# A hybrid decoder layer on one core: the output projection reads its activations by token halves, in pairs of tiles, and its two accumulators end one weight tile apart

## The chip, the cores and the metric

The kernel runs on one core of a Trainium2 chip. The metric is the time of one execution in microseconds, taken on the device; a lower time is better. Before the change three runs gave 2685.09, 2686.59 and 2689.0 us, a median of 2686.59 us.

## The reference

The kernel computes one decoder layer on `x` of 2048 tokens by 1024 columns, all in float32: two recurrent mixers side by side on the columns of one projection, an output projection of both with the residual added, and a feed-forward block. The output projection is the second line from the end of the loop.

```python
h    = rmsnorm(x, norm1_w)
proj = h @ w_in                                    # 1024 -> 3840 columns
o_hg = hgrn2_mixer(proj[:, :2048], ...)            # 4 heads of 128, chunks of 64 tokens
o_rw = rwkv7_mixer(token_shift(proj[:, 2048:]))    # 8 heads of 64
x    = x + concat([o_hg, o_rw]) @ w_out            # output projection and residual
x    = x + conv_ffn(rmsnorm(x, norm2_w), w_up, conv_w, conv_b, w_down)
return rmsnorm(x, final_norm_w)
```

## The kernel before

**Blocks and streams.** The 2048 tokens are four blocks of 512. A first phase runs the input projection, both mixers and the output projection of blocks 0 to 2; a second phase has the output projection of block 3 and the feed-forward block. The first phase is three streams of work: the dense one (projections, transposes, `out_block`), the RWKV-7 one (its products are in the PSUM tiles `rw`) and the HGRN2 one (`hg`). Each stream yields after a piece of work with a price in ns (680 for the piece of this change), and a scheduler places the pieces of all three among each other. So code that yields in another order gives every engine another order of instructions. Each engine works off its own list in that order: an instruction that waits holds all behind it. This holds for SP too, which issues most of the DMAs, and for POOL, which issues the loads of `w_out`.

**Products in three parts.** A float32 operand is split into a rounded part (a cast on ACT) and the remainder (a subtraction on DVE): `split_to` (L242, L243) for activations, `split` (L249, L250) for weights. `mm3` then makes three matmuls of it, high times high (L265), high times low (L266), low times high (L267). I call these three a triple.

**The output projection**, `out_block` (L373 to L409), of one block: the activations `oT` lie transposed in DRAM, 1024 rows (8 tiles of 128, index `k`) by 512 tokens. A block is four passes, named (i2, dh) here: token half `i2`, column half `dh`, in the order (0,0), (0,1), (1,0), (1,1). A pass has two PSUM tiles `accs` (tag `pj`, two buffers in all), one for each group of 128 tokens (`q` = 0, 1). For each of the 8 values of `k` it loads a 128x512 tile of `w_out`, splits it into `wh` and `wl` (four buffers each, as for the raw tile), and issues a triple for `q` = 0 and one for `q` = 1. At `k` = 6 it loads two tiles `xh` of the residual from `x` (L397). At the end DVE adds the two accumulators to them (L407), and SP stores them to `x1d` (L409). The next pass needs the same two PSUM buffers, so it begins when those additions are done.

**The activations.** In blocks 0 and 1 pass (0,0) loads a 128x512 tile `oraw` for each `k` (L386, in the buffers `sg`, of which there are two, shared with `xh` and with tiles of other streams), just ahead of the triple that reads it, and splits it into `hh` and `hl`. In block 2 the first token half was loaded earlier by `o_take` (L467 to L477) into a tile `ohl`; the second half is loaded by 128x256 tiles in pass (1,0), again one for each `k` just ahead of its triple. After pass (1,1) of blocks 0 and 1 `next_block` lets the transposes of another block overwrite `hh` and `hl`.

**The RWKV-7 rows that meet the change in block 2.** The stream makes a triangular inverse by transposes on DVE (`TZ` L789, `TTs` L795), products with it (L815, L828), casts on ACT to `M` and `UV` (L120), products with those (L848), and then a chain of eight steps in which the state `XH` goes from PE (L885) to DVE (L887) and back.

Of the kernel before, what the change touches and what calls it, by code (L numbers as in the profile page):

```python
# [18 lines left out]
P = 128  # L19
# [45 lines left out]
def tile_layer(ctx, tc, consts, x, norm1_w, w_in, hg_lb_logits, hg_norm_w, rw_shift_mu, rw_w0, rw_w2,  # L65
# [203 lines left out]
    def phase1(c1):  # L269
# [103 lines left out]
        def out_block(nb, oh=None, ol=None, then=None):  # L373


            for i2 in range(2):
                for dh in range(2):
                    accs = [bank("pj") for _ in range(2)]
                    for k in range(KD):
                        if i2 == 0 and dh == 0 and oh is None:  # L380
                            raw = stg("sg", "oraw", 2)
                            dma(raw, oT[nb][k * P:(k + 1) * P, :])
                            split_to(hh[:, k, :], hl[:, k, :], raw)
                        if i2 == 1 and dh == 0 and oh is not None:
                            raw = stg("sg", "oraw", 2)[:, 0:256]
                            dma(raw, oT[nb][k * P:(k + 1) * P, 256:512])  # L386
                            split_to(hh[:, k, 256:512], hl[:, k, 256:512], raw)
                        raw = wp.tile([P, 512], F32, tag="wraw", name="woraw", bufs=4)
                        wload(raw, w_out[0, k * P:(k + 1) * P, dh * 512:dh * 512 + 512])
                        wh, wl = split(wp, raw, [P, 512], "w", 4)  # L390
                        if k == KD - 2:
                            inputs = dh == 0 and (i2 == 0) == (oh is None)
                            xh = [wp.tile([P, BLK], F32, tag="wraw", name="xh", bufs=4) if inputs else
                                  stg("sg", "xh", 2) for _ in range(2)]
                            for q in range(2):
                                t0 = nb * BLK + (i2 * 2 + q) * P
                                dma(xh[q], x[0, t0:t0 + P, dh * 512:dh * 512 + 512])  # L397
                        for q in range(2):
                            is_ = slice((i2 * 2 + q) * P, (i2 * 2 + q + 1) * P)
                            lhs = ((hh[:, k, is_], hl[:, k, is_]) if oh is None or i2 == 1 else  # L400
                                   (oh[k // 4][:, k % 4, is_], ol[k // 4][:, k % 4, is_]))
                            mm3(accs[q], lhs, (wh, wl), k == 0, k == KD - 1)
                            if i2 == 1 and dh == 1 and q == 1:
                                next_block(then, k)
                            yield 680
                    for q in range(2):
                        V.tensor_add(xh[q], accs[q], xh[q])  # L407
                        r0 = (i2 * 2 + q) * P
                        dma(x1d[nb][r0:r0 + P, dh * 512:dh * 512 + 512], xh[q])  # L409
# [1165 lines left out]
```

## Time and profile before

| | |
|---|---|
| runs | 2685.09, 2686.59, 2689.0 us, median 2686.59 |
| profiled execution, its own time | 2686.26 us |
| its span in the profile | 2684.5 us |
| PE (TensorE) busy | 2614.7 us, 97% |
| PE weight loads | 2091.1 us, 78% (beside PE) |
| DVE (VectorE) busy | 1929.6 us, 72% |
| ACT (ScalarE) busy | 1338.3 us, 50% |
| POOL (GpSimd) busy | 381.8 us, 14% |
| output projection of blocks 0, 1 and 2 | from about 562 to 656, 909 to 1003 and 1247 to 1351 us of the span |

The span runs from the first to the last instruction recorded; the profiled execution's own time has 1.8 us more around it. In rows of groups and of the timeline, `out<-in` are the program's tiles, `L265` is a line of the kernel, and what stands in brackets is the engine's idle time ahead of the instruction and what ended it. "PEclk" is the clock that TensorE was granted, 1.00 being full.

### The profile page before, as it was taken

To read this page: it belongs to the slowest core of one execution; us is meant where nothing else is said; L and a number is where in the kernel's file an instruction comes from. 1 tells how busy PE (TensorE), PEld (TensorE's weight loads), DVE (VectorE), ACT (ScalarE), POOL (GpSimd) and SP (SyncE) were. 2 spreads that over 40 slices of the span, in tenths; PEclk is the share of its full clock that TensorE was granted. 3 is DMA by queue.
4 is the path that set the end of the run, shared out by engine and by line. 5 is a ranking of instruction groups with operands and counts; after the bars stand their busy time and mean duration, and the time that the engine had idled before them with its cause. 6 is when DMAs were issued, how large, how long until landed. Compare 5 with 4: busy or idle time off the path is not lost.

```text
span 2684.5 us, 47831 instructions
## 1 busy us (share of the span) xinstructions
PE 2614.7 (97%) x18059; PEld 2091.1 (78%) x18059; DVE 1929.6 (72%) x3705; ACT 1338.3 (50%) x2158; POOL 381.8 (14%) x684
## 2 busy tenths in 40 slices
PE   7999999999999999999999999999999999999998
PEld 5777777777777777778778888887888888788887
DVE  4867757576466764657578789988998888676556
ACT  4555442454544545433357665456555545445444
POOL 6433222212222123222100000000000000000000
PEclk9999999999999999999899999999999999999999
DMA  8654543355643556834584458756764463898665
GB/s 304 198 166 162 166 135 117 115 161 195 197 149 116 157 161 214 290 115 132 160 272 149 134 184 267 243 171 194 259 200 149 149 202 124 311 325 282 203 192 184
DMA packets 312828, 510.52 MB, mean 190 GB/s; under 512 B 46879, under 2 KB 143509, under 8 KB 312597
## 3 DMA queue, kind: packets, MB, share of 16 engines
q1 hardware_dynamic: 258225, 329.65, 37.2%
q0 software_dynamic: 54304, 177.80, 20.3%
q8 instruction: 142, 2.33, 0.4%
q14 instruction: 89, 0.73, 0.1%
q10 hardware_dynamic: 68, 0.02, 0.0%
HBM read 373.13 MB, written 134.22 MB: 189 GB/s over the span
## 4 chain that ended last, share of the span: by engine, by line
PE 74%; DVE 7%; DMA 6%; issue 6%; ACT 5%; POOL 1%; SPq 0%; DVEq 0%; POOLq 0%; ACTq 0%
PE pj L265 8%; PE pj L266 7%; PE pj L267 7%; PE ua L265 5%; PE ua L267 5%; PE ua L266 5%; PE da L266 3%; PE da L267 3%; PE da L265 3%; PE ud L266 2%; PE ud L265 2%; PE ud L267 2%; PE hg L969 2%; PE db L265 2%; PE db L266 2%
## 5 line engine op out<-in xcount | busy, mean ns | idle before, releaser
L265 PE MATMUL pj<-hh,wh 128*128 128x512 f32 x960 | 404.1, 421 | 4.5 <-ACT rkv L120 1.7
L266 PE MATMUL pj<-hl,wh 128*128 128x512 f32 x960 | 377.9, 394 | 0.0
L267 PE MATMUL pj<-hh,wl 128*128 128x512 f32 x960 | 377.7, 394 | 0.0
L265 PE MATMUL ua<-Bh,uwh 128*128 128x512 f32 x704 | 275.9, 392 | 1.0 <-ACT m L120 0.9
L267 PE MATMUL ua<-Bh,uwl 128*128 128x512 f32 x704 | 274.3, 390 | 0.0
L266 PE MATMUL ua<-Bl,uwh 128*128 128x512 f32 x704 | 274.1, 389 | 0.0
L265 PEld LDWEIGHTS pj<-hh,wh 128*128 128x128 f32 x960 | 181.2, 189 | 59.6 <-issue 14.0
L267 PEld LDWEIGHTS pj<-hh,wl 128*128 128x128 f32 x960 | 181.0, 189 | 40.1 <-issue 0.6
L266 PEld LDWEIGHTS pj<-hl,wh 128*128 128x128 f32 x960 | 181.5, 189 | 38.7 <-issue 5.9
L249 ACT CAST uwh<-uraw 128x512 fp32r<-128x512 f32 x220 | 135.1, 618 | 138.0 <-PE ua L266 63.2
L250 DVE TENSOR_TENSOR dal<-draw,dah 128x512 fp32r<-128x512 f32 x138 | 95.3, 690 | 113.1 <-ACT dah L249 113.0
L250 DVE TENSOR_TENSOR uwl<-uraw,uwh 128x512 fp32r<-128x512 f32 x220 | 147.3, 686 | 34.8 <-ACT uwh L249 34.8
L249 ACT CAST dah<-draw 128x512 fp32r<-128x512 f32 x138 | 85.8, 622 | 167.3 <-PE da L266 78.7
L265 PEld LDWEIGHTS ua<-Bh,uwh 128*128 128x128 f32 x704 | 132.2, 188 | 29.8 <-ACT m L120 2.4
L267 PEld LDWEIGHTS ua<-Bh,uwl 128*128 128x128 f32 x704 | 132.2, 188 | 28.1 <-DVE uwl L250 0.4
L266 PEld LDWEIGHTS ua<-Bl,uwh 128*128 128x128 f32 x704 | 132.2, 188 | 26.6
L265 PE MATMUL ud<-Bh,uwh 128*128 128x512 f32 x352 | 138.0, 392 | 0.0
L267 PE MATMUL ud<-Bh,uwl 128*128 128x512 f32 x352 | 137.0, 389 | 0.0
L266 PE MATMUL ud<-Bl,uwh 128*128 128x512 f32 x352 | 137.0, 389 | 0.0
L1445 POOL DMA_DIRECT2D gd<-y x2 | 1.1, 556 | 947.0 <-DVE y L1443 947.0
L266 PE MATMUL da<-dbl,dah 128*128 128x512 f32 x332 | 129.5, 390 | 1.1 <-DVE dbl L250 1.1
L267 PE MATMUL da<-dbh,dal 128*128 128x512 f32 x332 | 129.2, 389 | 0.0
(570 smaller groups left out, 6199.2 us busy)
## 6 DMA issues: line engine op xcount, KB each, us to landing
uraw<-in_w_up_dram SPq DMA_DIRECT2D x176, 256.0 KB, 3.3
woraw<-in_w_out_dram POOLq DMA_DIRECT2D x96, 256.0 KB, 3.4
br<-gd SPq DMA_DIRECT2D x88, 256.0 KB, 4.1
draw<-Sg SPq DMA_DIRECT2D x88, 256.0 KB, 3.0
draw<-Tw SPq DMA_DIRECT2D x88, 256.0 KB, 3.5
gd<-y SPq DMA_DIRECT2D x86, 256.0 KB, 2.8
Sg<-br SPq DMA_DIRECT2D x72, 256.0 KB, 2.6
xt<-x1d SPq DMA_DIRECT2D x32, 512.0 KB, 5.9
```

The costliest lines, as they stand in the source:

```text
L249: S.copy(hi, src)
L250: V.tensor_sub(lo, src, hi.bitcast(F32))
L265: TE.matmul(acc, lh, rh, start=first, stop=False, skip_group_check=skip)
L266: TE.matmul(acc, lh, rl, start=False, stop=False, skip_group_check=skip)
L267: TE.matmul(acc, ll, rh, start=False, stop=last, skip_group_check=skip)
L969: TE.matmul(o, kt[:, t0:t0 + 64], qs, start=True, stop=True, tile_position=(0, e * 64))
L1445: (dma if end is None else nc.gpsimd.dma_start)(gd_[2 * h + b][fb * P:(fb + 1) * P, :], ys[0][:, b * BLK:(b + 1) * BLK])
```

## The change

In `out_block` three things change. After the change every line behind the middle of the function has a number one or two off: L407 becomes L405, L409 becomes L407, and the lines of the mixers are one higher (L885 becomes L886).

1. The activations come in pairs of `k`, as tiles of 128x2x256, by token halves. In blocks 0 and 1 the first half is loaded in pass (0,0), pairs 0 and 1 at `k` = 0, pair 2 at `k` = 2, pair 3 at `k` = 4; the second half is loaded in pass (0,1), pairs 0 to 3 at `k` = 0 to 3, while pass (1,0) reads it. In block 2 only the second half is loaded, in pass (0,1) too.
2. The accumulator of `q` = 1 goes one weight tile behind that of `q` = 0: triples (0,k) and (1,k-1) alternate, and the pass ends with (0,7), (1,6), (1,7). A list `ws` keeps the weight tile of `k`-1. The addition and the store of each accumulator follow right on its last triple.
3. `xh` has a `wraw` buffer only in pass (0,0) of blocks 0 and 1; in block 2 all its tiles now come from `sg`.

```diff
                     accs = [bank("pj") for _ in range(2)]
+                    ws, first_pass = [], oh is None and i2 == 0 and dh == 0
+                    pairs = {0: (0, 1), 2: (2,), 4: (3,)} if first_pass else {m: (m,) for m in range(4)}
                     for k in range(KD):
-                        if i2 == 0 and dh == 0 and oh is None:
-                            raw = stg("sg", "oraw", 2)
-                            dma(raw, oT[nb][k * P:(k + 1) * P, :])
-                            split_to(hh[:, k, :], hl[:, k, :], raw)
-                        if i2 == 1 and dh == 0 and oh is not None:
-                            raw = stg("sg", "oraw", 2)[:, 0:256]
-                            dma(raw, oT[nb][k * P:(k + 1) * P, 256:512])
-                            split_to(hh[:, k, 256:512], hl[:, k, 256:512], raw)
+                        if i2 == 0 and (dh == 1 or oh is None):
+                            hs = slice(256 * dh, 256 * dh + 256)
+                            for m in pairs.get(k, ()):
+                                raw = stg("sg", "oraw", 2).rearrange("p (k t) -> p k t", k=2)
+                                dma(raw, oT[nb][2 * m * P:(2 * m + 2) * P, hs].rearrange("(k p) t -> p k t", p=P))
+                                split_to(hh[:, 2 * m:2 * m + 2, hs], hl[:, 2 * m:2 * m + 2, hs], raw)
                         raw = wp.tile([P, 512], F32, tag="wraw", name="woraw", bufs=4)
                         wload(raw, w_out[0, k * P:(k + 1) * P, dh * 512:dh * 512 + 512])
-                        wh, wl = split(wp, raw, [P, 512], "w", 4)
+                        ws.append(split(wp, raw, [P, 512], "w", 4))
                         if k == KD - 2:
-                            inputs = dh == 0 and (i2 == 0) == (oh is None)
-                            xh = [wp.tile([P, BLK], F32, tag="wraw", name="xh", bufs=4) if inputs else
+                            xh = [wp.tile([P, BLK], F32, tag="wraw", name="xh", bufs=4) if first_pass else
                                   stg("sg", "xh", 2) for _ in range(2)]
...
-                        for q in range(2):
+                        for q, kq in ((0, k), (1, k - 1), (1, k if k == KD - 1 else -1)):
+                            if kq < 0:
+                                continue
                             is_ = slice((i2 * 2 + q) * P, (i2 * 2 + q + 1) * P)
-                            lhs = ((hh[:, k, is_], hl[:, k, is_]) if oh is None or i2 == 1 else
-                                   (oh[k // 4][:, k % 4, is_], ol[k // 4][:, k % 4, is_]))
-                            mm3(accs[q], lhs, (wh, wl), k == 0, k == KD - 1)
-                            if i2 == 1 and dh == 1 and q == 1:
+                            lhs = ((hh[:, kq, is_], hl[:, kq, is_]) if oh is None or i2 == 1 else
+                                   (oh[kq // 4][:, kq % 4, is_], ol[kq // 4][:, kq % 4, is_]))
+                            mm3(accs[q], lhs, ws[kq], kq == 0, kq == KD - 1)
+                            if kq == KD - 1:
+                                V.tensor_add(xh[q], accs[q], xh[q])
+                                r0 = (i2 * 2 + q) * P
+                                dma(x1d[nb][r0:r0 + P, dh * 512:dh * 512 + 512], xh[q])
+                            if i2 == 1 and dh == 1 and q == 1 and (kq == k or k < KD - 1):
                                 next_block(then, k)
                             yield 680
-                    for q in range(2):
-                        V.tensor_add(xh[q], accs[q], xh[q])
-                        r0 = (i2 * 2 + q) * P
-                        dma(x1d[nb][r0:r0 + P, dh * 512:dh * 512 + 512], xh[q])
```

**What this moves on the engines.** Outside three stretches, those of the three blocks, the order is the same. PE has the same instructions. Three places in block 2 follow.

On PE, at the end of pass (0,1) before the change, the last steps of the RWKV-7 chain (L885) stand together, with the small products L895 and L969 between them, ahead of the first triple of pass (1,0). The number at a tile's name is that of the buffer; 64x64 x4 is four matmuls of that size.

```order
L969 MATMUL hg_14217<-hX_14188 64x32 x6
L885 MATMUL rw_13863<-XH_13861,M_13012 64x64 x4
L969 MATMUL hg_14217<-hX_14188 64x32 x2
L895 MATMUL rw_14012<-AR_12937,XH_13861 64x64 x2
L885 MATMUL rw_13863<-XH_13861,M_13012 64x64 x4
L895 MATMUL rw_14012<-AR_12937,XH_13861 64x64 x2
L885 MATMUL rw_13863<-XH_13861,M_13012 64x64 x4
L895 MATMUL rw_14012<-AR_12937,XH_13861 64x64 x2
L885 MATMUL rw_13863<-XH_13861,M_13012 64x64 x4
L895 MATMUL rw_14012<-AR_12937,XH_13861 64x64 x5
L265 MATMUL pj_14152<-wh_14160,hh_209 128x512
```

After the change the same pass ends thus; the accumulator of `q` = 0 (pj_13786) ends two triples ahead of that of `q` = 1 (pj_13787), and the next pass's pj_14168 begins.

```order
L265 MATMUL pj_13786<-wh_14141,ohl_12966 128x512
L266 MATMUL pj_13786<-wl_14142,ohl_12966 128x512
L267 MATMUL pj_13786<-wh_14141,ohl_12966 128x512
L265 MATMUL pj_13787<-wh_14115,ohl_12966 128x512
L266 MATMUL pj_13787<-wl_14116,ohl_12966 128x512
L267 MATMUL pj_13787<-wh_14115,ohl_12966 128x512
L265 MATMUL pj_13787<-wh_14141,ohl_12966 128x512
L266 MATMUL pj_13787<-wl_14142,ohl_12966 128x512
L267 MATMUL pj_13787<-wh_14141,ohl_12966 128x512
L886 MATMUL rw_13881<-XH_13879,M_13012 64x64 x4
L265 MATMUL pj_14168<-wh_14172,hh_209 128x512
```

The steps of the chain have moved from a cluster to single steps between triples (this one is the third of the eight, and the later ones stand between triples of pass (1,0) in the same way).

On ACT, at the RWKV-7 casts of pass (0,1) before the change: the casts of `M` and `UV` follow directly on `TTs`, and four weight casts follow on them.

```order
L120 ACTIVATE TTs_205<-rw_13724 32x8x32 x4
L120 ACTIVATE M_13012<-rw_13797 128x8x64
L120 ACTIVATE M_13012<-rw_13798 64x8x64 x2
L120 ACTIVATE UV_13179<-rw_13797 64x4x128 x2
L120 ACTIVATE UV_13179<-rw_13798 64x4x128 x2
L249 CAST wh_14002<-woraw_14000 128x512
L249 CAST wh_14090<-woraw_14088 128x512
```

After the change the same place reads:

```order
L120 ACTIVATE TTs_205<-rw_13732 32x8x32 x4
L242 CAST hh_209<-oraw_13788 128x2x256
L120 ACTIVATE M_13012<-rw_13801 128x8x64
L120 ACTIVATE M_13012<-rw_13802 64x8x64 x2
L120 ACTIVATE UV_13179<-rw_13801 64x4x128 x2
L120 ACTIVATE UV_13179<-rw_13802 64x4x128 x2
L242 CAST hh_209<-oraw_13850 128x2x256
L242 CAST hh_209<-oraw_13866 128x2x256
L249 CAST wh_14015<-woraw_14013 128x512
```

The first cast of the activations stands ahead of `M`, and two more stand between `UV` and the next weight cast.

On SP, around the end of pass (0,0) of block 2 after the change: the loads of `oraw` stand between the stores of `xh`, in the two `sg` buffers that those stores free.

```order
L396 DMA xh_13711<-in_x_dram 128x512
L396 DMA xh_13712<-in_x_dram 128x512
L407 DMA x1d2_148<-xh_13711 128x512
L386 DMA oraw_13788<-oT2_144 128x2x256
L407 DMA x1d2_148<-xh_13712 128x512
L386 DMA oraw_13850<-oT2_144 128x2x256
L386 DMA oraw_13866<-oT2_144 128x2x256
L386 DMA oraw_13957<-oT2_144 128x2x256
```

Before the change the loads of block 2 stood one pass later, behind the stores of pass (0,1), and singly:

```order
L409 DMA x1d2_148<-xh_14106 128x512
L409 DMA x1d2_148<-xh_14107 128x512
L1157 DMA uraw_14615<-oT3_145 128x512
L1157 DMA uraw_14631<-in_w_out_dram 128x512
L386 DMA oraw_14154<-oT2_144 128x256
L386 DMA oraw_14170<-oT2_144 128x256
```

So each store is now followed by a load that has to wait for the buffer of that store, and the pair of loads is a pass earlier.

## Prediction

> **What bounds the kernel now.** I read the busy table first, then the chain that ended last, by engine.
>
> ```profile
> span 2684.5 us, 47831 instructions
> PE 2614.7 (97%) x18059; PEld 2091.1 (78%) x18059; DVE 1929.6 (72%) x3705; ACT 1338.3 (50%) x2158; POOL 381.8 (14%) x684
> PE 74%; DVE 7%; DMA 6%; issue 6%; ACT 5%; POOL 1%; SPq 0%; DVEq 0%; POOLq 0%; ACTq 0%
> ```
>
> TensorE is busy for 97% of the span and is 74% of the chain. The change takes no matmul away, so it can win only PE's idle time and PE's time at a low clock, and only in the three stretches where the output projection runs. Those I cut out with the windows view: block 0, 1, 2.
>
> ```profile
> core 0: us, PE busy (x) PEld busy (x) DVE busy (x) ACT busy (x) POOL busy (x), PEclk, DMA share, GB/s
> 562.00:656.00 94.00, 89.11 (x985) 65.13 (x983) 73.58 (x169) 51.35 (x88) 16.36 (x31) 1.00 0.49 151
> 909.00:1003.00 94.00, 89.32 (x990) 66.34 (x989) 72.78 (x165) 51.85 (x88) 17.25 (x32) 1.00 0.48 154
> 1247.00:1351.00 104.00, 96.35 (x1057) 75.84 (x1055) 73.91 (x186) 47.69 (x86) 16.90 (x31) 0.93 0.44 140
> ```
>
> PE's idle time is 4.89 + 4.68 + 7.65 = 17.2 us, and only block 2 has a clock below 1.00. So 17.2 us and some of the clock is all there is to win. DVE is not idle either: three quarters of each stretch are its work. The waits view of PE over the whole run says what ends the idle time:
>
> ```profile
> PE pj L265 <- ACT hh L242: 6.4, 5, 2.2
> PE pj L265 <- DVE xh L407: 2.6, 4, 1.0
> PE rw L885 <- DVE XH L887: 1.4, 3, 0.6
> PE rw L848 <- ACT UV L120: 6.5, 6, 2.0
> ```
>
> (Total, times, longest.) The first two rows are exactly what the change touches: a triple that waits for its freshly split activations, and a pass that waits for the additions of the pass before. The third and fourth belong to the RWKV-7 stream, which is interleaved. PE's timeline in block 2 shows three of these waits together:
>
> ```profile
> 1301.88 0.50 PE L265 MATMUL pj<-wh,ohl 128*128 128x512 f32 x1
> 1303.83 0.39 PE L267 MATMUL pj<-wh,ohl 128*128 128x512 f32 x1
> 1308.13 0.45 PE L885 MATMUL rw<-XH,M 64*64 64x64 f32 x8 [0.23 <-DVE XH L887]
> 1309.33 0.45 PE L885 MATMUL rw<-XH,M 64*64 64x64 f32 x8 [0.63 <-DVE XH L887]
> 1310.39 0.45 PE L885 MATMUL rw<-XH,M 64*64 64x64 f32 x8 [0.50 <-DVE XH L887]
> 1312.70 0.79 PE L265 MATMUL pj<-wh,hh 128*128 128x512 f32 x1 [1.32 <-ACT hh L242]
> 1314.14 0.63 PE L265 MATMUL pj<-wh,hh 128*128 128x512 f32 x1
> 1317.13 0.63 PE L266 MATMUL pj<-wl,hh 128*128 128x512 f32 x1
> 1328.77 0.50 PE L265 MATMUL pj<-wh,hh 128*128 128x512 f32 x1 [2.23 <-ACT hh L242]
> ```
>
> Pass (0,1) ends at 1303.83; until 1312.70 PE has only small products and waits; the first large matmuls behind that run at half pace. From 1301.88 to 1303.83 are eight steps, 0.24 us each; from 1314.14 to 1317.13 seven, 0.43 us each.
>
> **The change part by part.** *Activations a pass ahead.* A split pair costs ACT and DVE this much, beside the weights:
>
> ```profile
> L242 ACT CAST hh<-oraw x24: 396/608/622, 569.0 to 1328.8; 128x512 fp32r<-128x512 f32 x16, 128x256 fp32r<-128x256 f32 x8
> L243 DVE TENSOR_TENSOR hl<-oraw,hh x24: 418/676/693, 569.7 to 1330.0; 128x512 fp32r<-128x512 f32 x16, 128x256 fp32r<-128x256 f32 x8
> L407 DVE TENSOR_TENSOR xh<-pj,xh x24: 666/684/692, 592.0 to 1349.9; 128x512 f32<-128x512 f32 x24
> L249 ACT CAST wh<-woraw x96: 600/619/626, 562.8 to 1343.8; 128x512 fp32r<-128x512 f32 x96
> L250 DVE TENSOR_TENSOR wl<-woraw,wh x96: 644/686/695, 565.5 to 1347.0; 128x512 fp32r<-128x512 f32 x96
> ```
>
> Blocks 0 and 1 keep eight splits of 512 elements each; block 2 goes from eight of 0.40 and 0.42 us to four of 0.61 and 0.68 us, 0.8 us less on ACT and 0.7 us less on DVE, both beside PE, so worth nothing. What counts is when they are done. In blocks 0 and 1 half the splits leave pass (0,0), where they and the weight splits share DVE, for pass (0,1). In block 2 they no longer stand just ahead of their triples. I take the whole 6.4 us of the hh row as gone. Without the cover of a pass they would be back; that is a rival below. The other price is the DMA side, the same bytes:
>
> ```profile
> xh<-in_x_dram SPq DMA_DIRECT2D x32, 256.0 KB, 3.5
> oraw<-oT SPq DMA_DIRECT2D x20, 256.0 KB, 3.3
> oraw<-oT SPq DMA_DIRECT2D x8, 128.0 KB, 2.5
> ```
>
> Eight issues of 256 KB stay eight in blocks 0 and 1 with rows half as long; eight of 128 KB become four of 256 KB in block 2. SP issues less, by four. The queue is 0.44 to 0.49 busy in these stretches, so I put nothing down, with the pair-shaped loads of the next paragraphs as the bound.
>
> *The lag of one weight tile.* It costs no instruction. At a pass's end the accumulator of `q` = 0 has two more triples behind it, 6 x 0.24 = 1.4 us, in which its addition of 0.68 us can run; its bank is then free for the next pass. The longest wait for L407 is 1.0 us, so all 2.6 us go, if DVE takes the addition up at once. What is late next is the addition of `q` = 1, but that accumulator is needed again only behind two triples of the next pass. Gain 2.6 us, and 0 at the other end.
>
> *The cluster.* In the rows of order the last steps of L885 go from a cluster to single steps between triples: each step's way through DVE then lies under 0.7 us of a triple or more. Gain the 1.4 us of the XH row. And with large matmuls all along I expect the slow stretch to go: 12 matmuls from 1312.70 at 0.43 instead of 0.24 us, 12 x 0.19 = 2.2 us (estimate from the two spacings).
>
> ```profile
> 1304.00:1311.40 7.40, 6.01 (x135) 4.93 (x134) 6.60 (x20) 1.45 (x3) 0.54 (x1) 0.96 0.87 269
> 1311.40:1318.00 6.60, 5.30 (x14) 4.14 (x15) 3.00 (x7) 1.38 (x3) 0.00 (x0) 0.52 0.68 214
> ```
>
> The drop comes right at the end of the stretch with small products and waits: 0.96 up to 1311.40, then 0.52.
>
> [...]
>
> Sum of what goes: 6.4 + 2.6 + 1.4 + 2.2 = **12.6 us**.
>
> *What comes back.* In block 2 the first pair's load now waits for the store of `xh`, and its cast stands ahead of the casts of `M` and `UV` on ACT, which works in order. The trip from a store through the reload to the split is in the trace, at the end of pass (0,1):
>
> ```profile
> 1304.68 0.92 SPq L409 DMA_DIRECT2D x1d<-xh  x2
> 1308.35 1.93 SPq L386 DMA_DIRECT2D oraw<-oT  x2
> ```
>
> From 1304.68 to the matmul that waited for the cast, 1312.70, it is 8.0 us, with 0.68 for the addition ahead 8.7. What it has to fit in, on DVE, ACT and PE at the end of pass (0,0):
>
> ```profile
> 1274.47 2.89 DVE L795 STREAM_TRANSPOSE TTs<-TZ 32x512 f32<-32x512 f32 x4
> 1277.60 1.27 DVE L407 TENSOR_TENSOR xh<-pj,xh 128x512 f32<-128x512 f32 x2
> 1280.57 3.40 PE L828 MATMUL rw<-RHS,TTs 64*64 64x128 f32 x64
> 1284.03 1.81 ACT L120 ACTIVATE M<-rw 128x512 f32<-128x512 f32 x3 [4.29 <-PE rw L828]
> ```
>
> ACT sat idle for 4.29 us ahead of `M`, since L828 ended only then. The addition of `q` = 0 now comes up to 2.89 us ahead of its old place, at about 1274.5; 8.7 us later is 1283.2, and then comes `M`. Between 0 (it just fits) and 6.2 us (a load as slow as the row in the last rival) I take 1.0. The addition ahead of the transposes delays them, and L815 and L828 behind them: between 0 and 0.7 us; I take 0.7, since nothing else feeds them. A weight tile is now held for two more triples, so the four buffers let splits run only two weights' worth ahead of the lagging triple where it was three: a new weight needs 0.62 + 0.69 = 1.3 us and loses 1.4 us of lead. Between 0 and 1.4, I take half, 0.7. Last, small products and triples change places all along, and the RWKV-7 waits with them; the nearest row is the one for UV, 6.5 us in six waits, and I take one more of them, 1.1 us, between a gain of 1.1 and a loss of 2.2. Together 1.0 + 0.7 + 0.7 + 1.1 = 3.5 us.
>
> Net 12.6 - 3.5 = 9.1 us, from the profiled execution's own 2686.26 us (the span and 1.8 us around it) **2677.2 us**. That execution lies 0.33 us below the median of 2686.59, well under what counts here.
>
> **The rivals.** *The clock stays low.* For it: block 2 keeps its bursts of 64x64 and 64x128 products, and the drop followed on one with PE mostly busy. Against: it came with the large matmuls missing for 9 us, and there will be triples in between. The 2.2 us stay: 2679.4.
>
> *The waits move to the RWKV-7 chain.* Its steps go through DVE and ACT, and the part of the projection with most splits has DVE nearly full:
>
> ```profile
> 562.00:584.00 22.00, 20.02 (x220) 14.84 (x218) 20.87 (x60) 15.14 (x28) 1.62 (x3) 1.00 0.46 124
> ```
>
> With 20.87 of 22 us busy, an addition that stands earlier in DVE's list pushes something else. Against: over the whole stretch DVE has 20 us to spare, and the change takes splits from this very part. At half of the gain, 6.3 - 3.5 = 2.8 us: 2683.5, between 2681 and 2688.
>
> *It doesn't do what it says.* The additions stay behind other work in DVE's list and the banks are free no sooner; the hh casts are still last. Then about 2686. Against: PE's order has the two triples in between, 1.4 us.
>
> *Slower: the trips in block 2 stop ACT.* All four loads share two buffers with `xh`, and their casts stand ahead of `M`, `UV` and the weight casts. The trace has pair-shaped loads that took much longer, from 1085 to 1110 us, with the busy tenths of the DMA engines there in 40 slices:
>
> ```profile
> DMA  9899619179999999999999999999999999999999
> ...
> oraw<-oT SPq DMA_DIRECT2D x4, 256.0 KB, 9.5
> ```
>
> At 9.5 instead of 3.3 us each trip is 6.2 longer. One stands ahead of `M`; two or three more, each waiting for a buffer of the one before, stand ahead of weight casts, whose lead is 0.7 us a triple. Three trips of 6.2 are 18.6 us without cover, with the other 2.5 us of my givebacks 21.1, less 12.6: 8.5 us slower, 2694.8. It makes the kernel slower by over 0.2% when the loss passes 12.6 + 5.4 = 18.0 us, nearly all of it uncovered. Against: there the DMA engines were full (nines nearly throughout), and here their share is 0.44.
>
> **How the numbers follow.** What a measurement of this kernel can tell from no change is about 0.2%, 5.4 us: below 2681.2 is faster, above 2692.0 slower. Chances: my forecast 0.45, the clock 0.18, the waits that move 0.22, nothing done 0.03, ACT stopped 0.12. The first two are faster, but for some 0.03 of them near the bound, with 0.01 of the third: 0.61. The third and fourth are nearly all within 0.2%, with the 0.03: 0.27. Slower 0.12. The range: at the low end all idle time of the three stretches, 2686.26 - 17.2 = 2669; at the high end the bound of the waits that move and of nothing done, 2687. The slower rival, and the little that might be won beyond the idle time through the clock, are left out.
>
> **What would show it.** In the profile after: the hh and L407 rows (L405 then) near 0 in PE's waits, and the PE busy share of the three windows up by 2 to 5 points; L886 as single steps between triples, without an idle time ahead; no clock of 0.5 behind the end of pass (0,1) of block 2. Wrong would be: new rows of PE waiting for `TTs`, `M` or `UV` in block 2 of over 2 us; ACT idle for `oraw` ahead of `M`; a row of PE waiting for `wh` or `wl` of more than 2 us; the slow clock at another place.

## The result, and the profile after

The changed kernel is slower. Its median is 2690.65 us (22 runs, 2682.26 to 2696.75), that of the kernel before, run beside it, 2685.51 us (22 runs, 2679.24 to 2692.78). The ratio is 1.0017 with a 95% interval of 1.0010 to 1.0025, that is 2.7 to 6.7 us more. I had forecast 9.1 us less.

The first two lines of the page after the change:

```profile
span 2688.8 us, 47809 instructions
...
PE 2623.3 (98%) x18059; PEld 2091.1 (78%) x18059; DVE 1928.2 (72%) x3701; ACT 1337.2 (50%) x2154; POOL 380.7 (14%) x684
```

The span grew by 4.3 us, but PE is busy for 8.6 us longer, with the same 18059 matmuls. So waits did go away, and more came back as busy time. The waits of PE over the whole run, after the change:

```profile
PE rw L849 <- ACT UV L120: 9.2, 7, 2.5
PE pj L265 <- DVE xh L405: 4.3, 3, 3.6
...
PE pj L266 <- DVE wl L250: 1.6, 6, 0.5
```

The row of 6.4 us for hh (L242) is gone, as forecast, and so is the row for XH. The row for the additions (L405, before L407) did not go: it is 4.3 us, one wait alone 3.6. The row for `UV` rose from 6.5 to 9.2 us.

To find the place I took the start of the same matmul, by its number in PE's list, in both traces. Where the order is the same the difference stays nearly constant (between blocks 1 and 2 it grows by 1.6 us); most of it arises in the three stretches. The same work, cut out by the windows view, before:

```profile
core 0: us, PE busy (x) PEld busy (x) DVE busy (x) ACT busy (x) POOL busy (x), PEclk, DMA share, GB/s
571.20:653.90 82.70, 78.51 (x925) 56.90 (x923) 62.98 (x137) 44.26 (x77) 14.04 (x26) 1.00 0.52 160
918.20:998.50 80.30, 76.67 (x918) 56.11 (x917) 59.42 (x126) 42.93 (x74) 14.03 (x26) 1.00 0.52 166
1252.00:1349.50 97.50, 90.84 (x1015) 71.68 (x1011) 67.52 (x168) 44.45 (x80) 15.70 (x30) 0.93 0.45 143
```

and after:

```profile
570.70:659.50 88.80, 83.89 (x925) 58.91 (x924) 62.52 (x136) 44.72 (x77) 13.95 (x26) 0.96 0.47 150
924.20:1009.10 84.90, 81.60 (x918) 57.77 (x917) 59.59 (x126) 42.73 (x73) 13.96 (x26) 0.98 0.50 157
1264.20:1354.90 90.70, 88.26 (x1014) 68.74 (x1011) 66.79 (x164) 45.00 (x77) 15.64 (x29) 0.98 0.48 154
```

Block 0 takes 6.1 us more, block 1 takes 4.6 more, block 2 takes 6.8 less. Look at PE's idle time, length minus busy: 4.2, 3.6 and 6.7 us before, 4.9, 3.3 and 2.4 after. In block 2 the forecast gain is there. In blocks 0 and 1 the idle time hardly changed, and PE is busy 5.4 and 4.9 us longer for the same matmuls. The rest, from the end of block 2 on, is a gain of 3.4 us at the start of the second phase and a loss of about the same behind it.

### The profile page after: what moved, and what is told of

Its sections match the earlier page's. It is cut to its first block, busy times and chain, and to the rows that moved or that the text cites. A ratio compares the mean times of both kernels' runs of the same rounds, so it can differ in the third digit from the quotient of the medians.

```text
span 2688.8 us, 47809 instructions
## 1 busy us (share of the span) xinstructions
PE 2623.3 (98%) x18059; PEld 2091.1 (78%) x18059; DVE 1928.2 (72%) x3701; ACT 1337.2 (50%) x2154; POOL 380.7 (14%) x684
## 4 chain that ended last, share of the span: by engine, by line
PE 80%; issue 5%; DVE 4%; DMA 4%; ACT 4%; POOL 1%; SPq 0%; POOLq 0%; DVEq 0%; ACTq 0%
PE pj L265 8%; PE pj L266 7%; PE pj L267 7%; PE ua L265 6%; PE ua L267 6%; PE ua L266 6%; PE ud L266 3%; PE ud L267 3%; PE ud L265 3%; PE da L266 3%; PE da L267 3%; PE da L265 3%; PE hg L970 2%; PE db L265 2%; PE db L266 2%
## 5 line engine op out<-in xcount | busy, mean ns | idle before, releaser
L265 PE MATMUL pj<-hh,wh 128*128 128x512 f32 x960 | 404.6, 422 | 8.2 <-ACT hh L120 2.8
L266 PE MATMUL pj<-hl,wh 128*128 128x512 f32 x960 | 378.3, 394 | 0.0
L267 PE MATMUL pj<-hh,wl 128*128 128x512 f32 x960 | 377.9, 394 | 0.0
L265 PE MATMUL ua<-Bh,uwh 128*128 128x512 f32 x704 | 276.8, 393 | 2.3 <-ACT uwh L249 1.5
L267 PE MATMUL ua<-Bh,uwl 128*128 128x512 f32 x704 | 274.6, 390 | 0.0
L266 PE MATMUL ua<-Bl,uwh 128*128 128x512 f32 x704 | 274.2, 390 | 0.0
L265 PEld LDWEIGHTS pj<-hh,wh 128*128 128x128 f32 x960 | 181.5, 189 | 63.2 <-issue 14.2
L267 PEld LDWEIGHTS pj<-hh,wl 128*128 128x128 f32 x960 | 181.2, 189 | 40.1 <-issue 0.6
L266 PEld LDWEIGHTS pj<-hl,wh 128*128 128x128 f32 x960 | 181.8, 189 | 38.6 <-issue 5.9
L265 PEld LDWEIGHTS ua<-Bh,uwh 128*128 128x128 f32 x704 | 132.3, 188 | 32.5 <-ACT m L120 3.8
L267 PEld LDWEIGHTS ua<-Bh,uwl 128*128 128x128 f32 x704 | 132.5, 188 | 28.1 <-DVE uwl L250 0.4
L266 PEld LDWEIGHTS ua<-Bl,uwh 128*128 128x128 f32 x704 | 132.4, 188 | 26.7
L265 PE MATMUL ud<-Bh,uwh 128*128 128x512 f32 x352 | 138.0, 392 | 0.0
L267 PE MATMUL ud<-Bh,uwl 128*128 128x512 f32 x352 | 137.0, 389 | 0.0
L266 PE MATMUL ud<-Bl,uwh 128*128 128x512 f32 x352 | 137.0, 389 | 0.0
L266 PE MATMUL da<-dbl,dah 128*128 128x512 f32 x332 | 129.5, 390 | 0.9 <-DVE dbl L250 0.9
L267 PE MATMUL da<-dbh,dal 128*128 128x512 f32 x332 | 129.2, 389 | 0.0
```

The lines of the kernel that those rows point to most:

```text
L265: TE.matmul(acc, lh, rh, start=first, stop=False, skip_group_check=skip)
L266: TE.matmul(acc, lh, rl, start=False, stop=False, skip_group_check=skip)
L267: TE.matmul(acc, ll, rh, start=False, stop=last, skip_group_check=skip)
```

## The experiments

The first question was which part of the change, and which block, makes the loss. My theories: **A**, the new loads make waits in blocks 0 and 1, which then halve the clock (my slower rival at another place); **B**, the lag spreads triples among small products, and each change between the two costs PE time. The count of changes is taken from PE's list: the number of times that small products stand between two large matmuls inside a stretch.

| kernel | changes in blocks 0, 1, 2 | block 0, us | block 1, us | ratio to before, interval |
|---|---|---|---|---|
| before | 26, 27, 20 | 82.7 | 80.3 | |
| changed kernel | 35, 33, 25 | 88.8 | 85.0 | 1.0017, 1.0010 to 1.0025 |
| e1, lag only | 40, 38, 26 | 89.5 | 84.6 | 1.0040, 1.0027 to 1.0053 |
| e2, loads only | 23, 25, 22 | 83.2 | 81.8 | 0.9982, 0.9970 to 0.9993 |
| e3, block 2 only | 26, 27, 25 | 81.4 | 80.3 | 0.9973, 0.9959 to 0.9986 |
| e4, blocks 0 and 1 only | 35, 33, 20 | 88.1 | 86.5 | 1.0059, 1.0044 to 1.0073 |
| e5, loads of block 2 only | 26, 27, 22 | 81.9 | 80.0 | 0.9981, 0.9972 to 0.9991 |
| e6, lag, coarse yield | 34, 31, 24 | 86.9 | 86.6 | 1.0024, 1.0012 to 1.0035 |
| e7, loads, coarse yield | 22, 20, 21 | 81.6 | 78.4 | 0.9965, 0.9953 to 0.9977 |
| e8, before, coarse yield | 23, 21, 21 | 83.4 | 78.2 | 0.9998, 0.9987 to 1.0010 |
| e9, three weight buffers | 40, 41, 22 | 108.6 | 102.8 | 1.0191, 1.0174 to 1.0209 |
| e10, loads, early additions, coarse yield | 22, 20, 21 | 81.7 | 79.3 | 0.9960, 0.9948 to 0.9973 |
| e11, changed kernel, fine yield | 43, 43, 22 | 89.7 | 88.5 | 1.0027, 1.0013 to 1.0042 |
| e12, before, order by pairs | 34, 34, 23 | 87.0 | 83.2 | 1.0030, 1.0013 to 1.0047 |

Block times are those of one profiled execution each, from the first matmul at which the changed list differs to the last; the ratios come from the timed runs. Differences in us below are those of the medians, if nothing else is said; what the interval of a ratio lies off 1, times 2686 us, is their interval. The runs hold both variants in one source, with the switches `lag` and `new` for each block; where a cut does not show a switch, it shows what the switch amounts to.

**e1, the lag alone.** The loads and the `xh` buffers of before, with the order of triples and the early additions of after:

```diff
-                        if i2 == 0 and (dh == 1 or oh is None):
-                            ...
+                        if first_pass:
+                            raw = stg("sg", "oraw", 2)
+                            dma(raw, oT[nb][k * P:(k + 1) * P, :])
+                            split_to(hh[:, k, :], hl[:, k, :], raw)
+                        if i2 == 1 and dh == 0 and oh is not None:
+                            ...
```

> All three blocks have the lagging accumulator and the early additions, and load and split the activations as before the change. Theory A (in blocks 0 and 1 the loads of the second token half put casts that wait for a DMA ahead of M and UV on ACT, and remainders ahead of the addition of xh on DVE; the waits this makes then halve the clock): blocks 0 and 1 have no hh cast waiting ahead of M, no wait for xh above 1 us, and each takes 0 to 2 us less than before (the xh waits of 2.6 us go), the whole about 2 us faster than before, at most 1 us slower. Theory B (the lag spreads the triples among the small products, and every change between the two costs PE about 0.24 us): blocks 0 and 1 have 6 to 9 changes more, as in the changed kernel, and each is 1.5 to 5 us longer; the whole 3 to 8 us slower.

Measured: 2695.24 us beside 2686.18, 9 us slower; blocks 0 and 1 are 6.8 and 4.3 us longer. Theory A falls as the main cause: none of the new loads is in this kernel. Block 1 is the clean case, since its clock is full and its idle time shorter than before (84.60 - 82.48 = 2.1 us, where before had 3.6):

```profile
926.50:1011.10 84.60, 82.48 (x918) 57.26 (x918) 59.83 (x126) 42.62 (x73) 13.98 (x26) 1.00 0.49 157
```

The same 918 matmuls keep PE busy for 82.48 instead of 76.67 us. How, PE's timeline of this kernel shows where it multiplies `UV` (64 products, L862 here):

```profile
947.71 1.68 PE L862 MATMUL rw<-UV,KBT 128*64 128x64 f32 x42 [0.78 <-ACT UV L120]
949.45 0.49 PE L265 MATMUL pj<-wh,hh 128*128 128x512 f32 x1
949.88 0.68 PE L862 MATMUL rw<-UV,KBT 128*64 128x64 f32 x14
950.48 0.50 PE L266 MATMUL pj<-wl,hh 128*128 128x512 f32 x1
950.82 0.40 PE L267 MATMUL pj<-wh,hl 128*128 128x512 f32 x1
951.15 0.45 PE L862 MATMUL rw<-UV,KBT 128*64 128x64 f32 x8
951.53 0.70 PE L876 MATMUL rw<-M 64*64 64x64 f32 x32
```

and in the kernel before, the same 64 products (L848):

```profile
938.54 2.27 PE L848 MATMUL rw<-UV,KBT 128*64 128x64 f32 x64 [0.97 <-ACT UV L120]
940.74 0.69 PE L862 MATMUL rw<-M 64*64 64x64 f32 x32
```

Before, 2.20 us in one piece. Here 947.71 to 951.53, 3.82 us, with three large matmuls in it that take 0.23 us each back to back (950.82 - 950.48, the first spacing behind a change, is 0.34). 3.82 - 0.69 - 2.20 is 0.93 us for two cuts, 0.47 us a cut. No idle time is shown at these places; a change looks like busy time.

What costs here is not the change of size. Where the small products are 128*128 in the rows, as the triples are, and not 128*64 or 64*64, a cut cost nothing, in this same kernel:

```profile
636.04 0.39 PE L265 MATMUL pj<-wh,hh 128*128 128x512 f32 x1
636.27 0.38 PE L1025 MATMUL hg<-ident,hk 128*128 128x128 f32 x2
636.41 0.48 PE L266 MATMUL pj<-wl,hh 128*128 128x512 f32 x1
636.72 0.39 PE L267 MATMUL pj<-wh,hl 128*128 128x512 f32 x1
```

From 636.04 to 636.72 is 0.68 us: two large matmuls at 0.23 and two small ones at 0.11 us, their median spacings in this trace, and nothing over. The trace before has seven such cuts in the stretches of the three blocks, around two to sixteen products of 128x128, with 0.01 to 0.03 us over in each; one, from 1259.97 to 1260.65, is 0.68 us like this one. The two cuts above, from 128*64 to 128*128 and back, are 0.47 us each. What TensorE does in that time was not shown.

Note also what is cut here: a single triple. L265 stands alone, L266 and L267 follow 1 us later. The stream yields only behind whole triples, so it did not ask for this cut; that the scheduler cut triples whose parts it did not yet expect to be ready is my reading, and e9 tests one side of it. The kernel before has such cuts too, only fewer.

**e2, the loads alone**, without the lag:

```diff
-                        for q, kq in ((0, k), (1, k - 1), (1, k if k == KD - 1 else -1)):
+                        for q, kq in ((0, k), (1, k)):
...
-                            if kq == KD - 1:
-                                V.tensor_add(xh[q], accs[q], xh[q])
...
+                    for q in range(2):
+                        V.tensor_add(xh[q], accs[q], xh[q])
```

> All three blocks load and split the activations as after the change, but the two accumulators end together, as before. Theory A: the long waits are there without the lag: PE waits 2 us or more in block 0 or block 1 for xh, M or UV, with the clock at half behind it, and those two blocks together are 5 to 11 us longer than before; block 2 is 3 to 7 us shorter. Theory B: blocks 0 and 1 are within 1 us of before, block 2 is shorter, and the whole is 3 to 7 us faster than before.

Measured: 2680.33 beside 2686.18 us, 0.18% faster; as theory B had it, with block 1 at 1.5 us more instead of at most 1. Theory A is not empty either: in block 1 PE waits 1.8 us for `UV` here, where before it waited 1.0. Two halves of one change thus pull apart, by -5.9 and +9.1 us (medians), and their sum of 3.2 us is near the 5.1 us of the whole.

**e3 and e4, by blocks**: the new code for block 2 alone, and for blocks 0 and 1 alone.

```diff
+            lag, new = {0: False, 1: False, 2: True}[nb], {0: False, 1: False, 2: True}[nb]
```

> Block 2 as after the change, blocks 0 and 1 as before it. Both theories place the loss in blocks 0 and 1: the whole is 6 to 11 us faster than before (block 2 took 7.3 us less in the changed kernel, and the start of the second phase 3.4 us less). The rival here, that the gain in block 2 was only where the windows of the clock happened to fall in that execution: within 3 us of before.

> Blocks 0 and 1 as after the change, block 2 as before it. If the loss lies in those two blocks whatever follows: 9 to 13 us slower than before (6.1 and 4.7 us longer in the changed kernel). If the lost time depends on the shift of the clock's windows alone: within 4 us of before.

Measured: 8.1 us faster and 15.1 us slower (medians). The first is as expected; the second has the expected sign and is 2 us above the range of 9 to 13 us, which its interval (11.8 to 19.6 us) overlaps. The gain is block 2's, the loss that of blocks 0 and 1.

**e5, which half makes the gain of block 2?** The new loads for block 2 alone, no lag anywhere.

```diff
+            lag, new = {0: False, 1: False, 2: False}[nb], {0: False, 1: False, 2: True}[nb]
```

> Only the loads and splits of block 2 as after the change (pairs, a pass ahead); no lag anywhere, blocks 0 and 1 as before. PE has 26, 27 and 22 changes from triples to small products in the three blocks, before the change 26, 27 and 20. If the earlier loads make the gain of block 2: that block is 4 to 9 us shorter than before, the whole 5 to 9 us faster. If the lag made it: block 2 within 2 us of before, the whole within 3 us.

Measured: 2680.53 beside 2686.25 us, 5.7 us faster. Block 2 took 91.8 us, 5.7 us less than before and 1.1 us more than in the changed kernel. Its window:

```profile
1250.30:1342.00 91.70, 88.60 (x1012) 69.28 (x1009) 66.30 (x164) 44.51 (x77) 16.04 (x30) 0.96 0.47 152
```

PE's idle time is 3.1 us where before had 6.7. The loads ahead make the gain; the lag is not needed for it. How large it is block 2's time alone does not say, since one execution's half clock is in it: before has 13.7 us of it there, this run 6.8. With the lag alone (e1) block 2 took 93.7 us, with 3.4 us at half clock and 4.0 us idle, and in e8, which has neither part of the change, 93.4 us with 3.4. The timed runs carry the claim (2.4 to 7.5 us by the interval).

**e6, e7, e8, the price of a change.** The stream yields after two triples instead of after each, so that small products come between them less often. With the lag alone (e6), with the loads alone (e7), and in the kernel before with nothing else (e8). For e7 and e8:

```diff
-                            yield 680
+                            if q == 1:
+                                yield 1360
```

> The lag alone, as in the first experiment, but the stream yields after two triples (price 1360) instead of after each, so that PE's list has 34, 31 and 24 changes instead of 40, 38 and 26. Price theory (every change costs 0.34 to 0.43 us, the slope over blocks 0 and 1 of the runs so far with idle time and half clock taken off): 15 fewer changes give 5 to 6.5 us back, so 2 to 5 us slower than before where the first experiment was 9 slower. Rival (the lag itself costs, by late buffers and additions, whatever stands between the triples): 8 to 10 us slower, as before.

> The loads of all three blocks as after the change, no lag, and the stream yields after two triples: 22, 20 and 21 changes, against 23, 25 and 22 in the second experiment. Price theory: 7 fewer changes, 2 to 3 us faster than that, so 7 to 10 us faster than before. Rival (changes cost nothing, coarse yields only delay the small products and so the recurrent chains): 3 to 6 us faster than before or less.

> The kernel before with nothing but the coarser yield: 23, 21 and 21 changes against 26, 27 and 20. Price theory: 8 fewer changes, 2.5 to 3.5 us faster than before. Rival: within 1.5 us of before, or slower, as the waits for hh and xh are all still there.

Measured: e6 5.8 us slower than before (e1 was 9.1 slower), between what the two theories said, and its interval (3.2 to 9.4 us) reaches into both; its block 1 ran at half clock for 10.2 us, which e1's had not. e7 8.8 us faster (6.2 to 12.6), as the price theory had it. e8 1.5 us faster, with an interval from 3.5 faster to 2.7 slower: the price theory's 2.5 to 3.5 did not show, but the interval tells nothing apart. Most of the waits for hh are still there (5.2 us, before 6.4).

Block 1 by itself, in the profiled executions in which its clock was full: 78.2 us with 21 changes (e8), 78.4 with 20 (e7), 80.0 to 80.3 with 27 (before, e3, e5), 81.8 with 25 (e2), 83.2 with 34 (e12), 84.6 with 38 (e1). A least-squares fit over before, after and e1 to e8, of the block's time without PE's idle time, on the changes and the time at half clock, gives 0.38 us a change in block 0 and 0.43 in block 1 (and 0.28 and 0.48 us for each us of half clock); no residual is over 1.0 us. The count has changes in it of the sort that cost nothing in the rows of e1, those whose small products are all 128*128 (3 to 6 in a block of these runs). Without them the fit gives 0.42 and 0.45 us a change, and its largest residual is 0.9 us.

**e9, where do the changes come from?** The lag holds each split weight for two triples more, in four buffers. So I took a buffer away without any lag, in the whole first phase (the input projection has the same edit).

```diff
-                        ws.append(split(wp, raw, [P, 512], "w", 4))
+                        ws.append(split(wp, raw, [P, 512], "w", 3))
...
```

> The kernel before, no lag and the old loads, with three instead of four buffers for the split weights in the whole first phase. PE's list then has 40, 41 and 22 changes in the three stretches, as many as with the lag alone (40, 38, 26), where before has 26, 27 and 20. Ring theory (the lag costs because it holds each weight for two more triples, which leaves the scheduler with triples that aren't ready, and it puts small products between their matmuls, 0.4 us each): block 0 takes 87 to 90 us and block 1 84 to 87 us, as in the first experiment, 11 to 14 us more for the two together than before, with PE's idle time there no larger than before by over 2 us; the whole is slower by that and by what the projections lose. Rival (the lag costs by what it does to the banks and additions): blocks 0 and 1 within 3 us of before.

Half of this came as expected. PE's list is cut as often as with the lag (40 and 41 changes), so a shorter lead of the weights is enough to make the scheduler cut triples. But the kernel lost far more, 53 us, with 16.0 and 12.8 us of idle time in blocks 0 and 1, and PE's waits say why:

```profile
PE pj L265 <- ACT wh L249: 25.0, 28, 1.2
```

With three buffers the weights are late in fact too, 28 times; in the changed kernel that row is 0.8 us. With its idle time and half clock taken off, e9 is still 4.6 and 3.7 us over the fit in blocks 0 and 1, which nothing here explains. e9 therefore shows what the lead does to the order, and does not measure the price.

**e10, the best parts together**: the new loads in all blocks, no lag, coarse yield, and each addition directly behind its accumulator's last triple.

> The loads as after the change, both accumulators of a pass on the same weight tile, each addition directly behind its accumulator's last triple, and a yield after two triples: 22, 20 and 21 changes as in the seventh experiment, which had the additions together at the end. If the earlier additions are worth something beside that: 1 to 3 us faster than the seventh, 10 to 12 us faster than before. If the addition of one accumulator is no earlier in time, as DVE works off its list in order: the same as the seventh, 7 to 10 us faster than before.

Measured: 2674.98 beside 2685.62 us, 0.40% faster (0.27 to 0.52). It is the fastest here, but its interval overlaps that of e7 (0.23 to 0.47), so what the earlier additions add is not settled. The fit, which did not see this run, is within 0.3 us of both its blocks.

**e11 and e12, two tests of the price** that leave loads and additions as they were. e11 is the changed kernel with a yield after each matmul. e12 is the kernel before with the triples in another order; since its hand-over counts only every second k, it makes five tiles of the next block's split activations twice and leaves three out, so what it computes is not the layer, and ACT and DVE have two splits more at the end of a block.

```diff
-                            mm3(accs[q], lhs, ws[kq], kq == 0, kq == KD - 1)
+                            TE.matmul(accs[q], lhs[0], ws[kq][0], start=kq == 0, stop=False)
+                            yield 227
+                            TE.matmul(accs[q], lhs[0], ws[kq][1], start=False, stop=False)
+                            yield 227
+                            TE.matmul(accs[q], lhs[1], ws[kq][0], start=False, stop=kq == KD - 1)
...
-                            yield 680
+                            yield 226
...
-                        for q, kq in ((0, k), (1, k)):
+                        for q, kq in (() if k % 2 == 0 else ((0, k - 1), (0, k), (1, k - 1), (1, k))):
```

> The changed kernel with nothing but a finer yield: after each matmul (227, 227, 226) instead of after each triple (680). PE's list has 43, 43 and 22 changes from triples to small products instead of 35, 33 and 25. Price theory (0.38 us a change in block 0, 0.43 in block 1, from a fit over ten runs): block 0 3 us, block 1 4.3 us longer than in the changed kernel, block 2 about 1 us shorter, the whole 4 to 8 us slower than the changed kernel, so 9 to 13 us slower than before. Rival (the loss belongs to the lag, and changes are only its companions): within 2 us of the changed kernel, 3 to 7 us slower than before.

> The kernel before with the triples of a pass in the order (0,k-1), (0,k), (1,k-1), (1,k) for every second k, both accumulators ending on the last weight as before, the additions at the end as before, old loads. It also holds weights longer, without any accumulator that ends early. PE's list has 34, 34 and 23 changes against 26, 27 and 20. Price theory: 8 x 0.38 + 7 x 0.43 + 3 x 0.4 = 7.3 us, so 5 to 10 us slower than before. Rival (the lagging end of the accumulators is the cause): within 3 us of before.

Measured: e12 8.0 us slower than before (3.5 to 12.6), in the expected range and outside that of its rival, with blocks 0 and 1 at 87.0 and 83.2 us; the fit, which did not see this run, gives 86.8 and 83.1 with its idle time (4.3 and 2.7 us) and half clock. e11 is 9.5 us slower than before by the medians, inside the range at its lower end; but its interval, 3.5 to 11.3 us, holds the rival's range too, so the timed runs of e11 do not decide. In its blocks the fit is within 0.3 us in block 0 (only 0.8 us longer than in the changed kernel, since the idle time fell from 4.9 to 2.2 us as the changes rose) and 1.7 us too high in block 1 (3.5 us longer, expected 4.3). That miss goes with the free changes: 8 of the 43 in block 1 have small products of 128*128 alone, and by the fit without such changes block 1 is 0.3 us off, and block 0 0.6.

The price holds in a kernel without the lag and without new loads (e12), so it belongs to the changes. One thing e12 shares with the changed kernel: its accumulator of `q` = 0 ends two triples ahead of the other. But its additions come at the end, as before, so no bank is free earlier.

## Why the prediction was wrong, point by point

**Activations a pass ahead: right, but their price was too low.** The hh row of 6.4 us is gone, and the loads alone are 0.18% faster (e2), with the coarser yield 0.35% (e7). For the RWKV-7 waits that change places I put down 1.1 us, at most 2.2; the row for `UV` rose by 2.7 us, from 6.5 to 9.2. That belongs to the loads: the row is 9.3 us in e2 and 6.6 us in e1.

**The lag of one weight tile: here the prediction failed.** "It costs no instruction" is true and was the wrong question. I counted instructions and waits, and gave the order of PE's list no price. This is the step that turned the sign: the sum has the lag as a gain of 2.6 us, less 0.7 for late weights, and by itself it made the kernel 9.1 us slower (e1). The lag takes the count of changes from 26 and 27 to 40 and 38 (e1), to 35 and 33 with the loads. At the fitted prices that is 9 x 0.38 + 6 x 0.43 = 6.0 us in blocks 0 and 1 of the changed kernel, of the 10.7 us that they lost; with 5 more changes in block 2, at 0.4, about 8 us in all (an estimate: the price in block 2 was not fitted). Of the 2.6 us that the lag was to win, the lag alone does win a part (in e1 that row is 1.2 us, no wait over 0.3); together with the loads, 4.3 us of waits for L405 stand in their place. The condition that I had named, that DVE takes the addition up at once, did not hold in block 0, as shown below.

**The cluster: its gain was paid back.** I took the spreading of L885 among triples as a gain of 1.4 us of XH waits. Those waits are gone, but each step that stands alone between triples is a change, at about 0.4 us; block 2 has 25 changes now instead of 20, about 2 us by that price.

**The ring of weights: right place, wrong effect.** I had the lead falling from three weights to two and put 0.7 us of late weights down. The rows for late weights did rise by about that, from 0.7 to 0.8 us for wh and from 0.9 to 1.6 for wl. The larger effect of the shorter lead I did not have: it changes the scheduler's list, as e9 shows by its order.

**The slower rival came, smaller than its price and not only in block 2.** I placed it in block 2, where the casts of hh stand ahead of `M`. It came there: ACT sat idle for the first pair ahead of `M`, and PE then waited 2.02 us for `UV`, where before it waited 0.19.

```profile
1294.73 0.62 ACT L242 CAST hh<-oraw 128x512 fp32r<-128x512 f32 x1 [3.29 <-DMA oraw<-oT]
1295.38 1.81 ACT L120 ACTIVATE M<-rw 128x512 f32<-128x512 f32 x3
...
1298.44 3.10 PE L849 MATMUL rw<-UV,KBT 128*64 128x64 f32 x64 [2.02 <-ACT UV L120]
```

L829, whose results `M` takes, was done at about 1293.5; `M` began at 1295.38, behind the cast. So the term that I put at 1.0 us, between 0 and 6.2, came to about 1.9. In block 1, too, ACT waited for `oraw` ahead of `M` (1.24 and 0.35 us), and PE then for `UV`, 2.53 us where before it waited 0.97:

```profile
944.64 2.61 PE L849 MATMUL rw<-UV,KBT 128*64 128x64 f32 x42 [2.53 <-ACT UV L120]
```

In block 0 the longest wait arose. There ACT waits for a load ahead of `M` and `UV`:

```profile
590.80 1.33 ACT L242 CAST hh<-oraw 128x512 fp32r<-128x512 f32 x2 [2.52 <-DMA oraw<-oT]
592.04 1.80 ACT L120 ACTIVATE M<-rw 128x512 f32<-128x512 f32 x3
```

on DVE the remainder waits for that cast, with the addition of `q` = 1 behind it in the list:

```profile
591.45 0.69 DVE L243 TENSOR_TENSOR hl<-oraw,hh 128x512 fp32r<-128x512 f32 x1 [2.38 <-ACT hh L242]
...
592.74 0.68 DVE L405 TENSOR_TENSOR xh<-pj,xh 128x512 f32<-128x512 f32 x1
```

and PE waits for that addition before it can go on with the next pass. I had this accumulator needed only behind two triples of the next pass; in the list one stood ahead of it (588.47 to 588.93).

```profile
589.26 0.56 PE L970 MATMUL hg<-hq,hk 128*64 128x64 f32 x10
593.47 0.80 PE L265 MATMUL pj<-wh,hh 128*128 128x512 f32 x1 [3.65 <-DVE xh L405]
```

So a wait of 3.65 us took the place of three waits of 1.0 us or less. I had said what is queued behind the casts on ACT, and not what is queued behind the remainders on DVE. In the sum this is small: PE's idle time in block 0 is 0.7 us more than before.

**The clock: right in block 2 by its number, the cause not shown, and lost again elsewhere.** In block 2's stretch 13.7 us at half clock became 3.4. But e8, with the old loads and no lag, also has 3.4 there, and e4, whose block 2 is that of before, 10.2; one execution each does not tell the spreading of the cluster from where the clock's pieces happened to fall. Blocks 0 and 1, which had none, got 6.8 and 3.4 us, at the fitted prices 1.9 and 1.6 us. The three half clocks in the blocks of the changed kernel begin at 592.7, 944.2 and 1299.2 us, within or just behind the long waits above (3.65 us up to 593.47, 2.53 up to 944.64, 2.02 up to 1298.44). Yet block 0 fell to half clock in e1 and e2 as well (for 6.8 and 10.2 us), without a wait of more than 1.1 us in either, so the new loads are not its only way there. Block 0 then adds up: 3.4 for changes, 1.9 for the clock, 0.7 idle, 6.0 of 6.1 us. Block 1 comes to 2.6 + 1.6 - 0.3 = 3.9 of 4.6; 0.7 us there is unexplained, within the fit's residuals. Both kernels are among the ten fitted, so this is bookkeeping; the test of the price is e12.

What stays open is the second phase: it gains 3.4 us at its start and loses them by small waits behind it. No experiment was made there.

## What to carry to other kernels

Where large matmuls and small tiled ones share TensorE, count in PE's own list how often they alternate, before and after a change; here each alternation cost about 0.4 us and showed as busy time, with no wait to read it from, but only where the small ones were 128*64 or less in the rows, and not 128*128 like the triples. Holding a buffer longer shortens the lead that a scheduler plans with, and it may pay by cutting work into pieces long before anything is late. Try the halves of a change apart: here the loads were worth about 6 us and the lag cost 9.

## What the runs showed of the hardware that was not expected

In the traces before and after the change the half clock comes in pieces of 3.41 us, or of two such (6.83 us, at three places), but for the last of each, which runs beyond the span, and on a grid: in both the starts lie multiples of 3.413 us apart. The expectations of e3 and e4 call these pieces the windows of the clock. Cut along that grid, the drops in the blocks follow pieces in which PE was busy for part of the time only. After the change:

```profile
589.20:592.60 3.40, 0.62 (x11) 0.42 (x10) 1.15 (x3) 1.70 (x3) 0.03 (x1) 1.00 0.71 264
592.60:599.40 6.80, 5.93 (x66) 4.63 (x66) 4.98 (x13) 4.61 (x9) 2.13 (x4) 0.50 0.57 180
940.80:944.20 3.40, 1.31 (x22) 0.92 (x20) 3.33 (x9) 3.20 (x6) 0.00 (x0) 1.00 0.52 171
944.20:947.60 3.40, 2.96 (x43) 2.71 (x43) 1.11 (x3) 3.18 (x6) 0.24 (x1) 0.50 0.16 55
1295.80:1299.20 3.40, 1.38 (x28) 0.95 (x28) 2.47 (x7) 3.30 (x7) 0.00 (x0) 0.99 0.58 170
1299.20:1302.60 3.40, 3.40 (x88) 3.28 (x88) 2.44 (x4) 2.49 (x5) 0.25 (x1) 0.50 0.16 42
```

and before:

```profile
1273.30:1276.70 3.40, 2.52 (x116) 1.61 (x116) 3.29 (x6) 1.94 (x6) 0.54 (x2) 1.00 0.66 214
1276.70:1283.50 6.80, 6.15 (x115) 5.24 (x106) 6.34 (x16) 2.17 (x6) 0.54 (x1) 0.50 0.44 134
1307.40:1310.80 3.40, 2.03 (x46) 1.58 (x47) 3.37 (x13) 0.83 (x2) 0.54 (x1) 1.00 0.93 295
1310.80:1317.60 6.80, 5.47 (x24) 4.22 (x21) 3.33 (x8) 1.38 (x3) 0.00 (x0) 0.50 0.73 234
```

In the pieces ahead of a drop PE is busy for 0.62 to 2.52 of 3.40 us. So such a piece need not be idle, and neither need it have one long wait: ahead of the drop at 1310.8 the longest is 0.63 us. The two longest idle stretches in the prediction's timeline of block 2, 1.32 us (up to 1312.70) and 2.23 us (up to 1328.77), are behind the drop. Being busy for so little of a piece was not enough by itself either: before the change a piece of the grid with PE busy for 2.35 us (222.0 to 225.4) was followed by one at full clock, and so was one with 1.74 us (672.6 to 676.0; PEclk is 1.00 from 676.0 to 679.4):

```profile
222.00:225.40 3.40, 2.35 (x17) 1.74 (x18) 3.40 (x5) 2.98 (x7) 1.05 (x2) 1.00 0.67 231
225.40:228.80 3.40, 3.20 (x21) 2.43 (x20) 3.40 (x7) 2.63 (x5) 1.29 (x2) 1.00 0.41 128
...
672.60:676.00 3.40, 1.74 (x9) 1.14 (x8) 1.67 (x5) 2.24 (x4) 1.07 (x2) 1.00 0.59 196
```

So in these traces PE's busy time alone does not tell when the clock drops, and what does was not measured.
